# Every second feed-forward residue by ScalarE and an accumulating DMA

## The chip, the cores and the metric

The kernel runs on one core of a Trainium2 chip. A core has a matrix engine (TensorE, PE in the profile), a vector engine (VectorE, DVE), an engine for activation functions (ScalarE, ACT), a general engine (GpSimd, POOL), an engine that issues transfers (SyncE, SP) and sixteen DMA engines that carry them out. Each engine works through its own queue in order and waits for the others by semaphores. Operands lie in the on-chip memory SBUF, 128 partitions wide; TensorE sums into banks of the memory PSUM. The metric is the time of one execution on the device, in microseconds; less is better.

## The reference

One layer of a streaming encoder on 256 tokens of width 2048, in float32. Its first part (attention and a convolution, joined by an output projection w_out) is left out here; the change touches the last lines, the feed-forward part with a hidden width of 5632:

```python
h = h + jnp.einsum('bsm,md->bsd', mixed, w_out[l].astype(mixed.dtype))
hn = rms_norm(h, norm2_g[l])
a = jnp.einsum('bsd,df->bsf', hn, w_gate[l].astype(hn.dtype))
bu = jnp.einsum('bsd,df->bsf', hn, w_up[l].astype(hn.dtype))
h = h + jnp.einsum('bsf,fd->bsd', jax.nn.silu(a) * bu, w_down[l].astype(hn.dtype))
```

## The kernel before

All products run on TensorE in a type of reduced precision (float32r). To keep float32's precision, each operand is split into a rounded part and a residue, hi + lo, and each product is summed from three: hi·hi, lo·hi and hi·lo. For the weights this split is made on the chip, chunk by chunk.

A chunk is two k-tiles (128 rows each) of 512 columns of a weight matrix: 128 partitions of 1024 values, 512 KB. There are 377 chunks; 113 belong to the input and output projections and the last 264 to the feed-forward part (w_gate, w_up and w_down, 88 each). The function split_chunk does four things with a chunk: SyncE loads it from the chip's main memory into a tile raw (line 270; five buffers), ScalarE rounds it into whi (line 275), VectorE subtracts whi from raw into wlo (line 276), and the price of that subtraction is taken off a credit by which other VectorE work is spread over the stream. whi and wlo have four buffers each.

The function multiply issues a chunk's twelve products: for each k-tile and each half of the tokens, first the two with whi (lines 306 and 307, eight products, the first half), then the four with wlo (line 312, the second half). A block of chunks (eight for w_gate and w_up; twelve and ten for the two rounds of w_down) sums into the same two PSUM banks. After a block a generator takes the sums over: silu_done (ScalarE, line 713), up_done (VectorE line 721, transposes on TensorE line 729, split of the result by ScalarE line 732 and VectorE line 733), or down_done, which adds into h on VectorE (line 746) and, in the second round, stores the result by SyncE (line 748). The order on every queue is written out by hand; there is no scheduler.

The feed-forward part runs in two rounds: six column blocks of w_gate and w_up, then four passes over w_down (twelve chunks each); then five column blocks and four passes (ten chunks each). run_chunks keeps each engine's queue ahead of TensorE: before the products of chunk t are issued, the chunks up to t + lead(t) have been given to split_chunk. lead is 1 at the very start and AHEAD = 2 after it. A tile that comes round again makes its writer wait until the last reader of its old contents is done: the load of chunk i waits for the subtraction of chunk i − 5, the rounding of chunk i for the products of chunk i − 4.

Of the kernel before, what the change touches and what calls it, by code (L numbers as in the profile page):

```python
# [12 lines left out]
F32 = mybir.dt.float32  # L13
F32R = mybir.dt.float32r
AF = mybir.ActivationFunctionType
# [22 lines left out]

# where the rows of the gains and biases begin, 128 values to a row
ROWS = (("norm1_g", "g1", KD), ("norm2_g", "g2", KD), ("subln_g", "sg", 2),  # L40
# [4 lines left out]

# k-tiles of 512 columns in a chunk of weights
NK = 2
# transposes that warm the tensor engine up
WARM = (14, 5)
# how x comes in: the k-tiles of its parts  # L50
XPARTS = (range(0, 2), range(2, 4), range(4, 8), range(8, 12), range(12, 16))
# channel tiles of the convolution per block of products
CONV_BLOCKS = (1, 1, 2, 2, 2)
# chunks of weights that are split ahead of their products
AHEAD = 2
RAW_BUFS = 5
AUX = 4
# resumptions between the steps of the q and k rows
LAG = (3, 2, 6)
HL_BUFS = 4  # L60
# what the vector engine's filler may take per resumption, and the price of its work
KTILE_US = 1.30
TAP_US = 0.396
CHAIN_US = 0.127
LO_US = 0.568
# feed-forward column blocks between two passes of w_down
FGROUPS = (6, 5)


def rope_constants():  # L70
    """cos and signed sin of the rotary angles, [S, 2, DH]."""
    inv = np.float32(THETA) ** (-np.arange(0, DH, 2, dtype=np.float32) / np.float32(DH))
    ang = np.arange(S, dtype=np.float32)[:, None] * inv[None, :].astype(np.float32)
    c, s = np.cos(ang), np.sin(ang)
    return np.ascontiguousarray(
        np.stack([np.concatenate([c, c], -1), np.concatenate([-s, s], -1)], 1).astype(np.float32)
    )
# [3 lines left out]
def tile_block(  # L81
# [16 lines left out]

    # ---------------------------------------------------------------- inputs and constants
    h = [const.tile([P, D], F32, tag=f"h{m}", name=f"h{m}") for m in range(NM)]  # L100
# [5 lines left out]

    # the tensor engine's clock rises while the first loads are under way
    def warm_up(n):
# [7 lines left out]
    act.dma_start(out=rows, in_=gains)  # L116
    # a first use of the activation table before anything waits for it
    act.copy(small.tile([P, 8], F32, tag="rsq", name="first"), neghalf)
# [26 lines left out]
    def late_constants():  # L145
        late_loads()
        yield from lag(4)
        pw = aux_ps.tile([P, N], F32, tag="aux", name="ps_cw")
        for ct in range(NCT):
            pe.transpose(pw[:, ct * W : (ct + 1) * W], cw_rows[ct * P // N][:, ct * P % N : ct * P % N + P], ident[:W, :W])  # L150
        act.copy(cw.rearrange("p c w -> p (c w)"), pw[:, : NCT * W])
        while not normed:
            yield
        yield from lag(16)
        act.mul(cols[:, AT["sg"] : AT["sg"] + 2], cols[:, AT["sg"] : AT["sg"] + 2], 1.0 - LAMBDA_INIT)
        # q is scaled by 1/sqrt(d) through its gain
        act.mul(gb[:, 0, :], gb[:, 0, :], 1.0 / math.sqrt(DH))
        hd = DH // 2
        for i, key in enumerate("qk"):
            for m in range(NM):  # L160
                t = const.tile([P, 2, DH], F32, tag=f"gcs{key}{m}", name=f"gcs{key}{m}")
                pool.tensor_tensor(t[:, 0, :], rt[:, m, 0, :], gb[:, i, :], ALU.mult)
                pool.tensor_tensor(t[:, 1, :hd], rt[:, m, 1, :hd], gb[:, i, hd:], ALU.mult)
                pool.tensor_tensor(t[:, 1, hd:], rt[:, m, 1, hd:], gb[:, i, :hd], ALU.mult)
                gcs[key, m] = t
        lp = pre.tile([P, 2, DH], F32, tag="att", name="lp", bufs=4)
        for i in range(2):
            pool.tensor_tensor(lp[:, i, :], lamv[:, 2 * i, :], lamv[:, 2 * i + 1, :], ALU.mult)
        yield from lag(4)
        dve.tensor_reduce(ls, lp, AX.X, ALU.add)  # L170
# [3 lines left out]
    def negative_lambda():  # L174
        """-lambda = exp(l2) - exp(l1) - lambda_init"""
        le = const.tile([P, 2], F32, tag="le", name="le")
        act.activation(le, ls, AF.Exp)
        pool.tensor_tensor(neg_lam, le[:, 1:2], le[:, 0:1], ALU.subtract)
        pool.tensor_scalar(neg_lam, neg_lam, 1.0, -LAMBDA_INIT, ALU.mult, ALU.add)

    def rsqrt_mean(dst, ss, n, eps):
        """dst = (ss / n + eps) ** -0.5 on a few columns."""
        k = dst.shape[-1]
        t = small.tile([P, 8], F32, tag="rsq", name="rsq")
        pool.tensor_scalar(t[:, :k], ss, 1.0 / n, eps, ALU.mult, ALU.add)  # L185
        pool.tensor_tensor(dst, t[:, :k], neghalf[:, :k], ALU.pow)  # L186
# [6 lines left out]
    def split_scaled(pair, src, scale):  # L193
        """hi + lo = src * scale, src in PSUM."""
        hi, lo = pair
        act.activation(hi, src, AF.Copy, scale=scale)  # L196
        dve.scalar_tensor_tensor(lo, src, scale, hi.bitcast(F32), ALU.mult, ALU.subtract)  # L197

    # ---------------------------------------------------------------- the stream of products
    # Beside it run generators, resumed after each k-tile: what they emit between two yields  # L200
    # is ready when they are resumed, so that no engine waits in its queue.
    running = []
# [12 lines left out]

    # banks of the aux pool that are read in a later stage than they are written
    held = [0]
# [5 lines left out]

    # work of the vector engine that fills what the stream leaves free
    side = []
# [3 lines left out]
    def spend(us):  # L229
        credit[0] -= us  # L230
# [6 lines left out]
    def side_step():  # L237
        """One step of the two oldest chains by turns: a step waits for the one before it."""
        two = side[:2]
        turn[0] += 1  # L240
        q = two[turn[0] % len(two)]
        spend(TAP_US if len(two) > 1 else TAP_US + CHAIN_US)
        q.popleft()()
        if not q:
            side.remove(q)
# [4 lines left out]
    def block(w, cols, ks, xs, done=None, bkey=None, first=True, last=True, spare=False, cuts=()):  # L250
        """Products of the k-tiles ks with columns of w, summed in two banks."""
        ks = list(ks)
# [12 lines left out]
    def split_chunk(w, k0, nk, cols, width, **_):  # L265
# [9 lines left out]
        act.copy(hi, raw)  # L275
        dve.tensor_tensor(lo, raw, hi.bitcast(F32), ALU.subtract)  # L276
        spend(LO_US * nk * width / N)
        return hi, lo

    def operand(xs, k):  # L280
# [4 lines left out]
        return pair  # L285

    accs = {}

    def multiply(c, hi, lo):
# [24 lines left out]
        if c is chunks[-1]:  # L314
            # one half of the tokens after the other, which shortens the end
            for m in range(NM):
# [30 lines left out]

    # ---------------------------------------------------------------- x, its transpose
    xT = {}
# [38 lines left out]

    # ---------------------------------------------------------------- convolution channels
    NB = N // P  # L390
# [6 lines left out]
    def glu_done(c0, nct, ps):  # L397
        """ps holds the gates of nct channel tiles, then what they gate."""
        w = nct * P
# [38 lines left out]

    # layer norm with tokens on partitions, and back
    ytok = {}  # L440
# [4 lines left out]
    def conv_back(b):  # L445
# [20 lines left out]
        yield  # L466
        # the table of the silu below, ahead of need
        act.activation(small.tile([P, 8], F32, tag="rsq", name="first"), neghalf, AF.Silu)
# [32 lines left out]

    # ---------------------------------------------------------------- attention
    v_sb = [pre.tile([P, H * E], F32, tag=f"v{m}", name=f"v{m}", bufs=1) for m in range(NM)]
# [18 lines left out]
    def qk_rows(key, b, m, ps):  # L522
        """Norm and rotation of the heads of block b, and their transpose."""
        G = N // DH
# [31 lines left out]
    def attend_scores(hd):  # L556
# [62 lines left out]
        pe.transpose(pt[:, 2, :], wts[1][:, P:], ident)  # L619
        # in the place of the head's q, which is done with  # L620
        wT = qkT["q"][:, 2 * hd : 2 * hd + 2, :].rearrange("p g s -> p (g s)")[:, : 3 * P].rearrange("p (k s) -> p k s", k=3)
# [46 lines left out]

    # ---------------------------------------------------------------- output projection
    hT = {}  # L670
# [32 lines left out]

    # ---------------------------------------------------------------- feed-forward
    ffn = {}
# [44 lines left out]

    # ---------------------------------------------------------------- the order of it all
    QC, KC, VC, AC, GC = 0, 1024, 2048, 3072, 4096
# [25 lines left out]

    lead = lambda t: 1 if t < len(XPARTS) else AHEAD
    for c, part in enumerate(XPARTS):  # L780
# [29 lines left out]
```

## Time and profile before

| what | us |
|---|---|
| median of 2 runs (1091.94 to 1092.33) | 1092.13 |
| span of the profiled execution | 1089.8 |
| TensorE busy (PE) | 1079.0 |
| VectorE busy (DVE), of it line 276 | 647.1, 456.4 |
| ScalarE busy (ACT), of it line 275 | 509.6, 390.8 |
| GpSimd busy (POOL) | 49.1 |

The span runs from the first to the last instruction of the profiled execution. Its first 375 us hold the projections, the convolution and attention; from there on the feed-forward part runs. Busy times of different engines overlap, so they don't add up to the span. Lines of the profile name the line of the kernel, the engine, the operation, the tile written and the tiles read, the count, the time in all and the mean of one in ns, and then how long the engine stood idle before these instructions and what ended that. Idle time of an engine that isn't the bottleneck costs nothing by itself. In the table of windows the columns are the busy time of each engine with the number of instructions, TensorE's granted clock, the mean busy share of the sixteen DMA engines and the bytes that they moved.

### The profile page before, as it was taken

To read this page: it belongs to the slowest core of one execution; us is meant where nothing else is said; L and a number is where in the kernel's file an instruction comes from. 1 tells how busy PE (TensorE), PEld (TensorE's weight loads), DVE (VectorE), ACT (ScalarE), POOL (GpSimd) and SP (SyncE) were. 2 spreads that over 40 slices of the span, in tenths; PEclk is the share of its full clock that TensorE was granted. 3 is DMA by queue.
4 is the path that set the end of the run, shared out by engine and by line. 5 is a ranking of instruction groups with operands and counts; after the bars stand their busy time and mean duration, and the time that the engine had idled before them with its cause. 6 is when DMAs were issued, how large, how long until landed. Compare 5 with 4: busy or idle time off the path is not lost.

```text
span 1089.8 us, 13224 instructions
## 1 busy us (share of the span) xinstructions
PE 1079.0 (99%) x4952; PEld 894.0 (82%) x4952; DVE 647.1 (59%) x828; ACT 509.6 (47%) x719; POOL 49.1 (5%) x77
## 2 busy tenths in 40 slices
PE   8999999999999999999999999999999999999998
PEld 7988888877888888888888888888888888888886
DVE  4799989898766544544545454444454454544443
ACT  6644566755754544434444343333443444433332
POOL 0030112210100100000000000000000000000000
PEclk9999999999999999999999999999999999999999
DMA  8756665554456557666575555556666656653654
GB/s 241 233 177 198 190 189 161 154 169 155 155 181 206 174 172 220 187 192 189 168 214 184 192 192 193 192 187 190 194 186 192 189 169 211 186 192 108 219 204 146
DMA packets 118733, 203.02 MB, mean 186 GB/s; under 512 B 6932, under 2 KB 28878, under 8 KB 118668
## 3 DMA queue, kind: packets, MB, share of 16 engines
q1 hardware_dynamic: 118608, 202.14, 59.7%
q8 instruction: 39, 0.64, 0.2%
q14 instruction: 26, 0.21, 0.1%
q10 hardware_dynamic: 60, 0.03, 0.0%
HBM read 200.04 MB, written 2.10 MB: 185 GB/s over the span
## 4 chain that ended last, share of the span: by engine, by line
PE 92%; DVE 3%; ACT 2%; POOL 1%; issue 1%; DMA 1%; SPq 1%; DVEq 0%; ACTq 0%
PE acc L307 30%; PE acc L312 30%; PE acc L306 30%; DVE y L431 1%; DVE wlo L276 1%; PE ps_a L729 1%; ACT whi L275 1%; DMA h<-in_x_dram 1%; PE ps_o L643 1%; ACT junk L355 0%; POOL rsq L185 0%; PE ps_h L686 0%; SPq L360 0%; POOL fq L186 0%; SPq L270 0%
## 5 line engine op out<-in xcount | busy, mean ns | idle before, releaser
L276 DVE TENSOR_TENSOR wlo<-raw,whi 128x1024 fp32r<-128x1024 f32 (+1 forms) x377 | 456.4, 1221 | 337.3 <-ACT whi L275 304.5
L275 ACT CAST whi<-raw 128x1024 fp32r<-128x1024 f32 (+1 forms) x377 | 390.8, 1051 | 366.4 <-PE acc L307 326.6
L306 PE MATMUL acc<-whi,hhi 128*128 128x512 f32 x704 | 274.8, 390 | 0.0
L307 PE MATMUL acc<-whi,hlo 128*128 128x512 f32 x704 | 274.1, 389 | 0.0
L312 PE MATMUL acc<-wlo,hhi 128*128 128x512 f32 x704 | 189.2, 391 | 0.0
L307 PEld LDWEIGHTS acc<-whi,hlo 128*128 128x128 f32 x704 | 132.2, 188 | 27.3
L306 PEld LDWEIGHTS acc<-whi,hhi 128*128 128x128 f32 x704 | 132.2, 188 | 27.2
L312 PEld LDWEIGHTS acc<-wlo,hhi 128*128 128x128 f32 x704 | 131.4, 188 | 26.8
L306 PE MATMUL acc<-whi,ahi 128*128 128x512 f32 x384 | 150.7, 392 | 0.0
L307 PE MATMUL acc<-whi,alo 128*128 128x512 f32 x384 | 150.5, 392 | 0.0
L306 PE MATMUL acc<-whi,xhi 128*128 128x512 f32 (+1 forms) x352 | 130.0, 376 | 2.8 <-ACT xhi L196 2.8
L307 PE MATMUL acc<-whi,xlo 128*128 128x512 f32 (+1 forms) x352 | 128.6, 372 | 0.5 <-DVE xlo L197 0.4
L431 DVE SCALAR_TENSOR_TENSOR y<-upad,cw,y 128x256 f32<-128x256 f32 x240 | 103.6, 481 | 3.5 <-ACT y L424 3.0
L312 PE MATMUL acc<-wlo,ahi 128*128 128x512 f32 x384 | 103.6, 391 | 0.0
L312 PE MATMUL acc<-wlo,xhi 128*128 128x512 f32 (+1 forms) x352 | 88.7, 377 | 1.4 <-DVE wlo L276 1.2
L306 PEld LDWEIGHTS acc<-whi,ahi 128*128 128x128 f32 x384 | 72.1, 188 | 15.9
L307 PEld LDWEIGHTS acc<-whi,alo 128*128 128x128 f32 x384 | 72.1, 188 | 15.3
L312 PEld LDWEIGHTS acc<-wlo,ahi 128*128 128x128 f32 x384 | 71.9, 188 | 15.6
L306 PEld LDWEIGHTS acc<-whi,xhi 128*128 128x128 f32 x352 | 66.5, 189 | 14.7 <-ACT xhi L196 3.2
L307 PEld LDWEIGHTS acc<-whi,xlo 128*128 128x128 f32 x352 | 66.6, 189 | 11.9 <-DVE xlo L197 0.9
L312 PEld LDWEIGHTS acc<-wlo,xhi 128*128 128x128 f32 x352 | 62.3, 190 | 13.0 <-DVE wlo L276 2.2
L733 DVE TENSOR_TENSOR alo<-ps_a,ahi 128x512 fp32r<-128x512 f32 x22 | 15.2, 691 | 46.0 <-ACT ahi L732 46.0
(138 smaller groups left out, 544.2 us busy)
## 6 DMA issues: line engine op xcount, KB each, us to landing
raw<-in_w_gate_dram SPq DMA_DIRECT2D x88, 512.0 KB, 4.4
raw<-in_w_up_dram SPq DMA_DIRECT2D x88, 512.0 KB, 4.5
raw<-in_w_down_dram SPq DMA_DIRECT2D x88, 512.0 KB, 4.2
raw<-in_w_in_dram SPq DMA_DIRECT2D x48, 512.0 KB, 3.7
raw<-in_w_out_dram SPq DMA_DIRECT2D x32, 512.0 KB, 3.7
raw<-in_w_in_dram SPq DMA_DIRECT2D x62, 256.0 KB, 3.6
h<-in_x_dram SPq DMA_DIRECT2D x6, 256.0 KB, 6.1
out_dram<-h SPq DMA_DIRECT2D x6, 256.0 KB, 2.5
```

What stands on the lines that cost most here:

```text
L275: act.copy(hi, raw)
L276: dve.tensor_tensor(lo, raw, hi.bitcast(F32), ALU.subtract)
L306: pe.matmul(ps[m], xhi[:, ms], hi[:, j, :], start=c["first"] and j == 0, stop=False)
L307: pe.matmul(ps[m], xlo[:, ms], hi[:, j, :], start=False, stop=False)
L312: pe.matmul(ps[m], xhi[:, ms], lo[:, j, :], start=False, stop=c["last"] and j == nk - 1)
L431: dve.scalar_tensor_tensor(y[:, ct, :], src, wk, y[:, ct, :], ALU.mult, ALU.add)
L643: pe.matmul(o[:, m, :], wT[:, (0 if m == 0 else 1 + k), :], v_sb[k][:, hd * E : (hd + 1) * E], start=k == 0, stop=k == m)
L729: pe.transpose(pt[:, i, m * P : (m + 1) * P], aa[m][:, c : c + P], ident)
L733: dve.tensor_tensor(lo, pt, hi.bitcast(F32), ALU.subtract)
```

## The change

For the chunks of w_gate, w_up and w_down, every chunk with an odd number (132 of the 264) gets its residue in another way: ScalarE writes −raw, rounded as whi is, into wlo, and a transfer issued by GpSimd adds raw to it, in place, inside SBUF. The other chunks keep the subtraction. A list counts the chunks given to split_chunk, and the credit isn't charged where VectorE isn't used. The look-ahead of the feed-forward chunks goes from 2 to 3. The rest of the diff takes comments away and moves no line ahead of line 276.

```diff
@@ split_chunk
         act.copy(hi, raw)
-        dve.tensor_tensor(lo, raw, hi.bitcast(F32), ALU.subtract)
-        spend(LO_US * nk * width / N)
+        if len(ready_order) % 2 and any(w is t for t in (w_gate, w_up, w_down)):
+
+            act.activation(lo, raw, AF.Copy, scale=-1.0)
+            pool.dma_start(out=lo, in_=raw.bitcast(F32R), accum_op=ALU.add)
+        else:
+            dve.tensor_tensor(lo, raw, hi.bitcast(F32), ALU.subtract)
+            spend(LO_US * nk * width / N)
+        ready_order.append(k0)
         return hi, lo
...
+    ready_order = []
     accs = {}
...
-    lead = lambda t: 1 if t < len(XPARTS) else AHEAD
+    lead = lambda t: 1 if t < len(XPARTS) else AHEAD + any(chunks[t]['w'] is m for m in (w_gate, w_up, w_down))
```

## The prediction

> **What bounds the kernel now.** I read the page first, then the groups and waits of the feed-forward stretch, the timelines of ScalarE, SyncE and TensorE, and last the table of windows.
>
> ```profile
> span 1089.8 us, 13224 instructions
> ...
> PE 1079.0 (99%) x4952; PEld 894.0 (82%) x4952; DVE 647.1 (59%) x828; ACT 509.6 (47%) x719; POOL 49.1 (5%) x77
> ...
> PE   8999999999999999999999999999999999999998
> ...
> PEclk9999999999999999999999999999999999999999
> DMA  8756665554456557666575555556666656653654
> ```
>
> TensorE works in every slice, at full clock. The chain of waits says the same.
>
> ```profile
> PE 92%; DVE 3%; ACT 2%; POOL 1%; issue 1%; DMA 1%; SPq 1%; DVEq 0%; ACTq 0%
> PE acc L307 30%; PE acc L312 30%; PE acc L306 30%; DVE y L431 1%; DVE wlo L276 1%; PE ps_a L729 1%; ACT whi L275 1%; DMA h<-in_x_dram 1%; PE ps_o L643 1%; ACT junk L355 0%; POOL rsq L185 0%; PE ps_h L686 0%; SPq L360 0%; POOL fq L186 0%; SPq L270 0%
> ```
>
> The products hold 90% of the chain; the residue's subtraction (L276) holds 1%. The groups and the waits of 400 to 1080 us, all feed-forward, show what the two side engines do there.
>
> ```profile
> L276 DVE TENSOR_TENSOR wlo<-raw,whi 128x1024 fp32r<-128x1024 f32 x245 | 297.2, 1224 | 281.5 <-ACT whi L275 249.0 <-PE acc L307 30.9
> L275 ACT CAST whi<-raw 128x1024 fp32r<-128x1024 f32 x244 | 254.9, 1053 | 315.0 <-PE acc L307 284.2 <-DMA raw<-in_w_down_dram 30.2
> ...
> L713 ACT ACTIVATE sil<-acc,rstd 128x512 f32<-128x512 f32 x20 | 12.6, 684 | 21.2 <-PE acc L312 21.2
> ```
>
> ScalarE's rounding (1.05 us) waits for TensorE to give a buffer back, and VectorE's subtraction (1.22 us) waits for ScalarE: both idle because TensorE is slower. On ScalarE's timeline the period of one chunk can be read.
>
> ```profile
> 503.85 1.05 ACT L275 CAST whi<-raw 128x1024 fp32r<-128x1024 f32 x1 [1.67 <-PE acc L307]
> 506.57 1.05 ACT L275 CAST whi<-raw 128x1024 fp32r<-128x1024 f32 x1 [1.67 <-PE acc L307]
> ```
>
> One chunk takes 2.72 us (506.57 − 503.85), twelve products of 0.227 us. The feed-forward part has 264 chunks, 718 us.
>
> **Where the DMA engines stand.** The change moves data, so their room decides. The last passes over w_down show them at full pace: SyncE holds the next loads behind the stores of the output, then issues them at once.
>
> ```profile
> 1003.66 0.95 SPq L748 DMA_DIRECT2D out_dram<-h  x2
> 1004.71 13.30 SPq L270 DMA_DIRECT2D raw<-in_w_down_dram  x10
> ```
>
> ```profile
> 1009.89 1.05 ACT L275 CAST whi<-raw 128x1024 fp32r<-128x1024 f32 x1 [9.10 <-DMA raw<-in_w_down_dram]
> 1011.24 1.06 ACT L275 CAST whi<-raw 128x1024 fp32r<-128x1024 f32 x1 [0.29 <-DMA raw<-in_w_down_dram]
> ...
> 1015.30 1.05 ACT L275 CAST whi<-raw 128x1024 fp32r<-128x1024 f32 x1 [0.30 <-DMA raw<-in_w_down_dram]
> ```
>
> ```profile
> 375.00:1085.00 710.00, 710.00 (x3166) 586.19 (x3165) 346.38 (x314) 288.85 (x297) 0.00 (x0) 1.00 0.60 187
> ...
> 1010.00:1015.00 5.00, 5.00 (x23) 4.10 (x23) 3.68 (x3) 4.11 (x4) 0.00 (x0) 1.00 1.05 399
> ```
>
> Here ScalarE waits for the loads, which land every 1.35 us ((1015.30 − 1009.89) / 4); the windows' last two columns give 399 GB/s at a share of 1.05, against 187 GB/s and 0.60 over the whole part. So all sixteen engines together need 1.355 us for one 512 KB chunk at their best, and 0.60 × 2.72 = 1.63 us at their usual pace. Two chunks take TensorE 5.44 us and the loads 2.71 us: 2.73 us per pair are free.
>
> **The change, part by part.** *Removed:* one subtraction for every odd chunk of the feed-forward part: 132 × 1.224 = 162 us of VectorE. It held 1% of the chain, and VectorE idles 281 us in that part already. Gain: nothing, since TensorE is busy without a break.
>
> *Added on ScalarE:* 132 sign-reversed copies of 128x1024. Not in the trace; the nearest rows are the rounding, 1.05 us, and two silu rows, 2 × 0.684 = 1.37 us from PSUM. I take 1.05, as source and size are the rounding's. ScalarE then needs 3 × 1.05 = 3.2 us of each 5.44 and idled 315 us: hidden. The copy waits until the products of four chunks before have read the residue buffer. Behind it stands the next rounding, which waits for the following chunk's first half anyway, and at block ends the silu, about 1.05 us later, with a chunk or more before its reader.
>
> *Added on the DMA queues:* 132 transfers of 512 KB inside SBUF, issued by GpSimd, which has no work left there (0.00 in the window). No transfer of GpSimd is in the trace. Issue: SyncE's costs 0.37 us, and GpSimd's own small operations about 1.1 us; either is far under 5.44.
>
> ```profile
> L186 POOL TENSOR_TENSOR fq<-rsq,neghalf 128x4 f32<-128x4 f32 x8 | 9.0, 1131 | 0.7
> ```
>
> ```profile
> L270 SPq DMA_DIRECT2D raw<-in_w_gate_dram x7: 367/368/368, 513.2 to 528.0; - x7
> ```
>
> The engine time is the term that decides. An accumulation reads raw, reads the residue tile and writes it back. The lower end is one load's time, 1.355 us, if the second read costs nothing. For the upper end the stores from SBUF serve:
>
> ```profile
> out_dram<-h SPq DMA_DIRECT2D x6, 256.0 KB, 2.5
> ...
> out_dram<-h SPq DMA_DIRECT2D x4, 128.0 KB, 2.0
> ```
>
> 128 KB more take 0.5 us more, so 512 KB take 2.0 us, and three passes one after another 6.0 us. Between these: two passes at the load's best pace, 2.71 us, and three, 4.07 us. I take the middle of the last two, 3.39 us, because both reads must pass, and because the load's pace is this kernel's best and not its usual one. The pair then needs 2.71 + 3.39 = 6.10 us of DMA against 5.44 of TensorE: 0.66 us too much, × 132 = 87 us.
>
> The Trainium skill ("DMA: Bandwidth & Descriptors", Issuing engines are not separate DMA queues) says that DMAs of the scalar, sync and gpsimd engines run on the same 16 DMA engines and interleave. It speaks against the change; no run here yet shows a GpSimd transfer beside SyncE's.
>
> *Moved:* the look-ahead of the feed-forward chunks goes from 2 to 3, so loads, roundings and residues stand one chunk earlier in every queue; at the stores SyncE passes one load more before it waits. The hidden accumulation has this cover: the rounding starts once the first eight products of the fourth chunk before are done (8 × 0.227 = 1.81 us), rounding and copy end 2.1 us later, 1.2 us into the next chunk, and the residue is read 1.81 us into its own: 3 × 2.72 + 1.81 − 1.2 = 8.8 us are there. A load takes this long from issue to landing:
>
> ```profile
> DMA to landing us min/median/max: 3.4/4.4/8.6
> ```
>
> The raw buffer is held until the accumulation has landed, and SyncE's queue stands behind it: the load five chunks later, and all loads after it, wait.
>
> ```profile
> SPq L270 <- DVE wlo L276: 510.4, 225, 6.6
> ...
> SPq L748 <- DVE h L746: 42.3, 6, 14.9
> ```
>
> SyncE waited for the subtraction in 225 loads (up to 6.6 us) and nobody suffered; it will wait for the transfer in half of them.
>
> *At the last three stores* the cover is thin. TensorE starts the chunks after a pass at these times:
>
> ```profile
> 1003.20 0.39 PE L306 MATMUL acc<-whi,ahi 128*128 128x512 f32 x1
> ...
> 1011.44 0.39 PE L306 MATMUL acc<-whi,ahi 128*128 128x512 f32 x1
> ...
> 1014.18 0.39 PE L306 MATMUL acc<-whi,ahi 128*128 128x512 f32 x1
> ```
>
> The fourth chunk after the pass (1011.44) is the first held load now; its rounding ends at 1009.89 + 1.05 = 1010.94, 0.5 us early. After the change the fifth is the first held. Passes have ten chunks and end on even numbers, so the fifth is odd, an accumulated one. Its copy ends at 1009.89 + 2 × 1.05 = 1012.0, its residue is due at 1014.18 + 1.83 = 1016.0. Its transfer, 3.4 us plus the 2.0 us by which the shortest landing exceeds 1.355, plus 1.1 of issue, takes 6.5: 2.5 us late, three times, 8 us. That is the price wherever the cover above is gone.
>
> Sum against the profiled execution: 1089.8 + 87 + 8 = 1185 us of span; the median of the runs, 1092.1, is 2.3 above the span, so 1187 us.
>
> **The rivals.** *1, the engines have room (not slower).* If the accumulation costs two passes at the load's best pace, the pair needs 5.42 us, under 5.44, and nothing but the three store gaps shows: 1092 + 8 = 1100 us, or 1092 without them. It decides up to 2.9 us per accumulation (0.17 × 132 = 22 us, 2%). For it: 399 GB/s were reached, and SBUF rows need no HBM. Against it: it needs the sixteen engines at their best all the time. The Trainium skill ("Collectives: The Full Stack", The bandwidth ceiling) says that a reduce is slow only by its two source reads, not by the add; by that it is this case, two passes. Chance 0.35; 0.01 more that the new branch is never taken, 1092.
>
> *2, the accumulation is much dearer*, over 4.1 us, because passes do not overlap or the add is slow. At 6.0 us the pair needs 8.7 us: 3.27 × 132 = 432, 1532 us with the gaps and the launch. For it: nothing in the trace shows an add in a DMA. Chance 0.16.
>
> *3, a round trip that is too long though the engines have room.* A residue buffer comes back every fourth chunk, 10.88 us; less the copy 1.05 and its reading 0.91, 8.9 are left. With the longest landing, 8.6, and 1.1 of issue, 0.8 us are missing per four chunks: 66 × 0.8 = 53 us, 1145 us. Against it: the median landing is 4.4. Chance 0.03.
>
> *4, faster by over 2%* would need shorter products, and TensorE has no gap to give: 0.01.
>
> **How the numbers follow.** My forecast (the DMA engines become the bound, 2.9 to 4.1 us per accumulation) has 0.44 and its own range is 1114 (1092 + 22) to 1277 (4.07: 1.34 × 132 = 177, plus 8). 2% is about what a measurement of this kernel can tell from no change. Same: 0.36 (rival 1 and the untaken branch). Slower: 0.44 + 0.16 + 0.03 = 0.63. The range begins below rival 1 at 1088 and reaches to 5.4 us per accumulation, (2.71 + 5.4 − 5.44) × 132 = 352, to 1450; beyond it lies about half of rival 2.
>
> **What would show it.** Right: a DMA share near 1 from 375 us on, ScalarE's rounding waiting for raw loads in place of L307, the load's landing well above 4.4 us, L312 waiting for the accumulation, chunks of about 3.05 us, VectorE's L276 at 245 instead of 377 instructions. Wrong: a share of 0.8 to 0.95 with TensorE at 99%, which is rival 1; a share under 1 with L312 waiting is rival 3; TensorE below 80% is rival 2. If the copy takes well over 1.4 us or GpSimd's issue over 2 us, those terms were mis-sized.

## The result, and the profile after

| | before | after |
|---|---|---|
| median of the runs, us | 1092.13 | 1117.55 (1117.2 to 1117.9, 2 runs) |
| span of the profiled execution, us | 1089.8 | 1116.0 |
| ratio of the times, 95% interval | 1 | 1.0241 [1.0224, 1.0258] |

The change makes the kernel 2.4% slower. The direction was forecast, the size was not: 25 us were lost and 95 forecast. These are the lines of the page after that answer to those shown of before. Line 276 is now 281, the copy is 278, the transfer 279, and the products' lines 306, 307 and 312 are 313, 314 and 319.

```profile
span 1116.0 us, 13501 instructions
...
PE 1089.1 (98%) x4952; PEld 895.4 (80%) x4952; DVE 488.4 (44%) x696; ACT 636.1 (57%) x851; POOL 159.0 (14%) x209
...
PE   8999999999999999999999999999999999998987
...
DMA  8756655544557999999999999999999999999995
...
q1 hardware_dynamic: 118608, 202.14, 52.9%
q0 software_dynamic: 19008, 69.21, 33.1%
...
PE 67%; DMA 20%; ACT 4%; DVE 4%; issue 3%; POOL 1%; SPq 1%; ACTq 0%; DVEq 0%
...
L279 POOL DMA_DIRECT2D wlo<-raw x132 | 114.1, 864 | 693.6 <-ACT wlo L278 678.7
...
L278 ACT ACTIVATE wlo<-raw 128x1024 fp32r<-128x1024 f32 x132 | 139.0, 1053 | 11.5 <-PE acc L319 11.5
...
wlo<-raw POOLq DMA_DIRECT2D x132, 512.0 KB, 7.1
raw<-in_w_gate_dram SPq DMA_DIRECT2D x88, 512.0 KB, 7.1
```

VectorE lost 159 us of work (647.1 − 488.4) and nobody gained by it. The DMA engines, 0.6 busy before, are busy for nine tenths or more in all but the first and the last slice of the feed-forward part, and a gate load lands 7.1 us after its issue in place of 4.4 (medians). Still TensorE is almost as busy as before until the 37th slice, which begins at 1004 us. The two rows of the wait table for its weight loads, asked for 375 to 985 us and for 985 us to the end, say what it waits for; the columns are the sum, the number and the longest.

```profile
PEld acc L319 <- DMA wlo<-raw: 13.6, 19, 1.5
```

```profile
PEld acc L319 <- DMA wlo<-raw: 11.6, 4, 4.2
```

It waits for the accumulated residue alone: nineteen short waits in 610 us, then four with the longest at 4.2 us. To see what each part cost, I read from the trace when TensorE begins the first feed-forward chunk (its first weight load, at 353.7 us before and 353.4 after), the 130th chunk (after one gate and one up block of the feed-forward part) and the 338th (the last forty, whose passes end in stores). From the first feed-forward chunk to the 130th is "entry", from there to the 338th "steady", then to the last product "last passes".

| kernel (profiled execution) | entry | steady | last passes | more than before |
|---|---|---|---|---|
| before | 44.5 | 576.5 | 111.2 | |
| after | 45.9 | 586.4 | 126.4 | 1.4 + 9.9 + 15.2 |

So two separate losses have to be explained: about 11 us spread over entry and steady part, and 15 us in the last 126.

**A late landing in the steady part.** In the groups of GpSimd, in the windows and on the timeline of TensorE's weight loads, one of the nineteen waits looks like this (the accumulated chunk that TensorE begins at 556.67):

```profile
550.37 0.86 POOL L279 DMA_DIRECT2D wlo<-raw  x1 [4.51 <-ACT wlo L278]
```

```profile
551.00:553.00 2.00, 2.00 (x10) 1.69 (x9) 0.00 (x0) 0.78 (x1) 0.23 (x1) 1.00 1.03 372
553.00:555.00 2.00, 2.00 (x10) 1.65 (x10) 1.23 (x1) 1.75 (x3) 0.00 (x0) 1.00 0.91 205
```

```profile
559.78 0.77 PEld L319 LDWEIGHTS acc<-wlo,hhi 128*128 128x128 f32 x4 [1.33 <-DMA wlo<-raw]
```

GpSimd is done with the issue at 551.23. The DMA engines are full (1.03, 0.91), but with something else: by the packet records of the two queues, from 551.23 to 555.1 they begin 526 packets of loads, two loads' worth, and none of the accumulation. Its last packet ends at 559.3, and it counts as landed 9.4 us after the issue began. TensorE could have used it from 558.45 on, 8.1 us after the issue began, and waits 1.33 us. These 8.1 us are also the median of what the order of work leaves an accumulation in the steady part, from the start of its issue until it is due.

**A stall at a store.** The chain of waits, in order of time (start, duration, what), around the first stall of the last passes:

```profile
1021.74 0.93 PE acc L319 x4
...
1023.71 1.06 ACT wlo L278
1024.77 0.28 issue
1025.06 5.84 DMA wlo<-raw
1030.89 0.04 issue
1030.94 2.07 PE acc L319 x4
```

The accumulation (5.84 us) ends the wait. Then the same four products take 2.07 us that took 0.93 before the wait: the granted clock is half of full for 3.41 us from 1030.5 on. It drops so three times, at 1030.5, 1064.6 and 1095.3. From the first weight load after each of the three long waits to the same one of the next chunk it takes 3.97, 4.22 and 4.01 us in place of 2.75: some 4.0 us for the clock. The waits of the weight loads are 11.6 us in this part (4.1, 4.2, 2.8 and 0.4), so together they make up the 15.2, 0.4 us over, since every wait holds a little of the usual gap.

### The profile page after: what moved, and what is told of

Its sections match the earlier page's. It is cut to its first block, busy times and chain, and to the rows that moved or that the text cites. A ratio compares the mean times of both kernels' runs of the same rounds, so it can differ in the third digit from the quotient of the medians.

```text
span 1116.0 us, 13501 instructions
## 1 busy us (share of the span) xinstructions
PE 1089.1 (98%) x4952; PEld 895.4 (80%) x4952; DVE 488.4 (44%) x696; ACT 636.1 (57%) x851; POOL 159.0 (14%) x209
## 4 chain that ended last, share of the span: by engine, by line
PE 67%; DMA 20%; ACT 4%; DVE 4%; issue 3%; POOL 1%; SPq 1%; ACTq 0%; DVEq 0%
PE acc L319 22%; PE acc L314 21%; PE acc L313 21%; DMA wlo<-raw 13%; DMA raw<-in_w_down_dram 4%; ACT wlo L278 2%; DMA raw<-in_w_gate_dram 1%; DVE wlo L281 1%; DVE y L438 1%; ACT whi L275 1%; PE ps_a L736 1%; DMA raw<-in_w_up_dram 1%; DMA h<-in_x_dram 1%; PE ps_o L650 1%; ACT junk L362 0%
## 5 line engine op out<-in xcount | busy, mean ns | idle before, releaser
L281 DVE TENSOR_TENSOR wlo<-raw,whi 128x1024 fp32r<-128x1024 f32 (+1 forms) x245 | 298.0, 1221 | 546.3 <-ACT whi L275 546.0
L279 POOL DMA_DIRECT2D wlo<-raw x132 | 114.1, 864 | 693.6 <-ACT wlo L278 678.7
L319 PEld LDWEIGHTS acc<-wlo,hhi 128*128 128x128 f32 x704 | 130.2, 188 | 37.1 <-DMA wlo<-raw 11.3
L278 ACT ACTIVATE wlo<-raw 128x1024 fp32r<-128x1024 f32 x132 | 139.0, 1053 | 11.5 <-PE acc L319 11.5
L319 PE MATMUL acc<-wlo,ahi 128*128 128x512 f32 x384 | 106.9, 401 | 10.7 <-DMA wlo<-raw 10.7
```

The lines of the kernel that those rows point to most:

```text
L278: act.activation(lo, raw, AF.Copy, scale=-1.0)
L279: pool.dma_start(out=lo, in_=raw.bitcast(F32R), accum_op=ALU.add)
L319: pe.matmul(ps[m], xhi[:, ms], lo[:, j, :], start=False, stop=c["last"] and j == nk - 1)
```

## The experiments

Two theories stood against the prediction's bandwidth theory once its size had failed. **Round trip:** the engines have room, but single accumulations land later than four buffers allow. **Held loads:** in the last passes the loads stand behind the stores, and the first of them is an accumulated chunk's. All kernels below start from the changed one unless said otherwise; each was timed against the kernel before, which took 1091.1 to 1091.4 us on these chips.

**What one accumulation costs the engines.** All residues accumulated, and a plain copy in the accumulation's place:

```diff
-        if len(ready_order) % 2 and any(w is t for t in (w_gate, w_up, w_down)):
+        if any(w is t for t in (w_gate, w_up, w_down)):
```

> All 264 feed-forward residues go through the accumulating transfer, so the DMA engines must become the bound and the time gives the engine time of one accumulation. Two passes at the load's best pace (2.7 us): chunks of 1.355 + 2.7 = 4.05 us, 264 x (4.05 - 2.72) = 351 us more than before, about 1443 us. The prediction's 3.39 us: chunks of 4.74 us, 534 us more, about 1626 us. Three passes (4.07 us): about 1806 us.

```diff
-            pool.dma_start(out=lo, in_=raw.bitcast(F32R), accum_op=ALU.add)
+            pool.dma_start(out=lo, in_=raw.bitcast(F32R))
```

> The odd chunks' transfer copies raw over the residue instead of adding it, so it reads one operand and not two; the residue is not computed. If the second read is what an accumulation costs beside a copy, a 4 KB packet takes about 164 ns in place of the 328 ns seen in the changed kernel, the pair of chunks needs 2.7 + 1.3 = 4.0 us of 5.44, the DMA share falls to about 0.8, the small waits of the steady part go (11 us) and the gaps at the three stores shrink by about 1.3 us each: 1097 to 1104 us. If the add or the path inside SBUF is the dear part and not the second read, packets stay well above 200 ns and the time stays above 1110.

Measured: 1395.3 us with all accumulated (ratio 1.2789 [1.2748, 1.2831]), under all three expected times, and 1099.5 us with the copy (1.0074 [1.0059, 1.0089]), as expected. The pages' rows of GpSimd's queue (packets, MB, share of 16 engines), of the former and the latter:

```profile
q0 software_dynamic: 38016, 138.43, 51.3%
```

```profile
q0 software_dynamic: 19008, 69.21, 18.2%
```

Before, a feed-forward chunk takes 2.77 us in the mean, transposes and w_down included ((44.5 + 576.5 + 111.2) / 264). With all accumulated it takes 2.77 + (1395.32 − 1091.16) / 264 = 3.92 us, of which one accumulation can hold no more than 3.92 − 1.355 = 2.6 us. By the packets' time it is 0.513 × 1392.6 / 264 = 2.71 us, and 0.331 × 1116.0 / 132 = 2.80 in the changed kernel; a copy takes 0.182 × 1098.3 / 132 = 1.51. An accumulation costs a little under two copies; whether the second read or the add is the dear part, these two runs don't separate. That is the first rival's price, not the 3.39 us of the forecast: a load pair and an accumulation need at most 2.71 + 2.6 = 5.3 us of TensorE's 5.44. With the copy, steady part and entry lose nothing (44.5 and 576.4) and the last passes still 9.0 us.

**Room to land.** Three ways to give more buffers:

> Seven raw buffers in place of five, seven pairs of whi and wlo in place of four (from the memory that is free in the feed-forward part) and a look-ahead of five chunks in place of three; the same transfers. Round trip theory: the engines have room (two passes, 5.4 of 5.44 us), and the loss comes from single accumulations that land 8 to 9 us after their issue, where four buffers leave about 8.1; with two more chunks of cover the stalls go, in the steady part and at the stores: 1092 to 1095 us. Bandwidth theory: the pair really needs over 5.44 us; deeper buffers only delay the first stall, the steady part still loses about 11 us: 1102 us or more.

The edit of the second way, five pairs, in parts:

```diff
-RAW_BUFS = 5
+RAW_BUFS = 3
...
-HL_BUFS = 4
+HL_BUFS = 5
...
+        own = "pool" in ffn and len(ready_order) % 9 in (0, 1, 3, 4, 6, 7)
+        raw = view(ffn["pool"].tile([P, NK * N], F32, tag="fraw", name="raw", bufs=6) if own
+                   else wp.tile([P, NK * N], F32, tag="raw", name="raw", bufs=RAW_BUFS))
...
-... AHEAD + any(chunks[t]['w'] is m for m in (w_gate, w_up, w_down))
+... AHEAD + (1 + ('pool' in ffn)) * any(chunks[t]['w'] is m for m in (w_gate, w_up, w_down))
```

> Five pairs of whi and wlo in place of four, at the same place in memory (three raw buffers there and six from free memory in the feed-forward part), and a look-ahead of four chunks: an accumulation has 2.7 us more to land, at the same transfers and the same pace of the products (2.72 us a chunk). Round trip theory: the steady stalls (11 us) and the three at the stores (15 us with the clock) go, 1092 to 1096 us. Bandwidth theory: the steady part still loses about 11 us, 1102 us or more.

> Nine raw buffers in place of five, all else as in the changed kernel. If accumulations are late because SyncE is held by the raw buffer that an accumulation still reads and then issues two or three loads in a burst, ahead of the next accumulation, the bursts go and most of the 11 us of the steady part: 1105 to 1110 us, with the store gaps unchanged. If the DMA engines simply serve what was issued first, more loads stand ahead of each accumulation and it gets no better: 1115 us or more.

| run | time, us | ratio, interval | entry, steady, last passes: more than before |
|---|---|---|---|
| seven pairs, elsewhere in memory | 1109.2 | 1.0167 [1.0152, 1.0183] | 2.8 + 8.6 + 6.7 |
| five pairs, same place | 1106.2 (1101.8 to 1107.4) | 1.0128 [1.0106, 1.0150] | 3.8 + 0.0 + 6.1 |
| nine raw buffers alone | 1131.4 | 1.0354 [1.0317, 1.0391] | 4.3 + 11.5 + 27.1 |

The times of the runs with seven and with five pairs both lie where the bandwidth theory had them, and for other reasons. With seven pairs, from 400 to 985 us the weight loads never wait for a residue; but the chunks of w_gate and w_up themselves take longer: 2.79 us for the odd ones, whose whi and wlo lie in the other place, and 2.75 for the even, against 2.72. A slower TensorE also leaves the DMA engines more time, so that run decides nothing. The run with five pairs keeps the operands where they were and the pace at 2.72. Windows of 400 to 980 us, first the changed kernel, then this one (the last columns are clock, DMA share and GB/s):

```profile
400.00:980.00 580.00, 574.71 (x2550) 469.75 (x2549) 157.88 (x151) 336.03 (x349) 88.58 (x103) 1.00 1.01 279
```

```profile
400.00:980.00 580.00, 580.00 (x2593) 479.45 (x2592) 162.80 (x155) 341.08 (x356) 90.37 (x105) 1.00 1.03 288
```

The same transfers at a DMA share of 1.03, and TensorE is busy for all 580 us: the steady loss is gone to the tenth. The landings of the accumulations in these windows, in the same order:

```profile
DMA to landing us min/median/max: 5.2/7.2/9.4
```

```profile
DMA to landing us min/median/max: 4.9/7.9/10.5
```

They come no earlier with five pairs, but they now have 10.9 us in the median and not 8.1. It was the round trip and not the bandwidth. (The profiled execution was the shortest of four, so the other runs may wait somewhere else too. The fifth pair and the fourth chunk of look-ahead were not tried apart.) What is left of the loss lies in the entry and the last passes.

The other raw buffers are not what helped: nine of them with four pairs made it worse, by little in the steady part (11.5 us against 9.9) and by much at the stores (27.1 against 15.2). After a store SyncE now issues nine loads one right after another, where the changed kernel issues five and then waits for a buffer, and the longest wait for a residue grows to 7.4 us. That fits "served in the order of issue". The bursts of held loads in the steady part this run did not take away: SyncE still waits for an accumulation at 108 loads there, 466.5 us in all (changed kernel: 108, 403.9), so it doesn't tell what they cost.

**The stores.** ScalarE issues them (sp.dma_start becomes act.dma_start for out):

> The stores of the output are issued by ScalarE, so SyncE's loads do not stand behind them. If the last passes lose their 15 us because the loads are held behind the stores (three stalls of 2.4 to 3.8 us on the accumulated residue and three drops of the granted clock after them), these go and the clock stays at 0.998: about 1102 us. If the last passes lose time because the DMA engines cannot keep up there, it stays at 1115 to 1118.

1107.0 us, 1.0147 [1.0132, 1.0163], 5 us more than expected. Entry and steady part stay as they were (1.8 + 9.5), the last passes lose 4.1 us in place of 15.2, and the clock doesn't drop. So the loads held behind the stores are the second loss; some 4 us are left because the waits for late residues go on there:

```profile
PEld acc L319 <- DMA wlo<-raw: 4.7, 4, 1.7
```

The even chunks in place of the odd ones:

> The even chunks are accumulated in place of the odd ones. The first load held behind a store then belongs to a subtracted chunk, and the accumulated one after it has 2.7 us more for 1.4 us more of loading. If the store gaps come from the accumulation's time on the first held chunk, they shrink by at least 1.3 us each and the clock drops go with most of them: 1105 to 1112 us. If not, 1115 to 1119.

1112.5 us, 1.0194 [1.0177, 1.0211]. Just outside the expectation, and not by the way expected: the last passes still lose 13.6 us with two clock drops. The accumulated chunk is now the second held one, and its stall after the first two of these stores shrinks as forecast, to 2.6 and 2.9 us from 4.1 and 4.2; but other waits come in, and the sum of the waits stays (11.3 us against 11.6). What improved is the steady part, 3.8 us in place of 9.9, for which I have no explanation.

**The look-ahead.** Left at 2 with the rest of the change, and at 3 in the kernel before, without accumulation:

> The look-ahead stays at 2 as before, the rest of the change stands. SyncE passes one load fewer before each store, and the silu of a block stands ahead of the next rounding. The accumulated chunk after a store gets its load 1.4 us later in the row of held loads: stalls of about 5 us in place of 3.3, 1121 to 1127 us in all. If the third chunk of look-ahead has no part in it, 1116 to 1119.

> The kernel before with the look-ahead of 3 in the feed-forward part and no accumulation. No theory gives it a cost or a gain: TensorE has no gap there to fill, 1090 to 1093 us. Over 1095 would mean that a part of the loss is the look-ahead's.

1150.6 us (1.0547 [1.0531, 1.0563]) and 1091.1 us (1.0001 [0.9992, 1.0010]). The look-ahead costs nothing by itself, and the change needs it: without it the steady part loses 32 us and the last passes 26. The expectation (1121 to 1127) looked at the stores alone and missed the steady part, where an accumulation one chunk later in every queue is late again and again: 31 waits of up to 2.5 us from 400 to 985 us, some for accumulations that are issued only 4.1 us before they are due.

**Everything at once, and half of it.** Five pairs, stores by ScalarE, and the longer look-ahead and the first accumulation only once the new buffers exist (three accumulations fewer); and, by itself, every fourth residue in place of every second:

> As the run with five pairs of whi and wlo, but with the stores issued by ScalarE, and with the longer look-ahead and the first accumulation only once the feed-forward buffers exist (two or three accumulations fewer). If the loss of the changed kernel is the sum of late landings in the steady part and of the loads held behind the three stores, nothing is left: 1092 to 1095 us. If the engines lack bandwidth anywhere, or accumulations slow the products, some of it stays: 1098 us or more.

> Every fourth residue is accumulated (66 in place of 132). Four chunks then need 4 x 1.355 + 2.7 = 8.1 us of the DMA engines against 10.9. Waiting behind loads shrinks with the load on the engines, so the steady part loses 0 to 3 us; of the three stores only the second has an accumulated chunk as the first held one (3.5 us and 1.7 us for the clock): 1093 to 1100 us. If each accumulation had a cost of its own, half of the loss stays: 1104 us.

1098.1 us (1.0064 [1.0047, 1.0081]), 3 us over what the sum of the two losses gave: the steady part loses nothing and the last passes 0.7 us, but the entry 5.0. The timelines of GpSimd and of the weight loads show where:

```profile
366.68 1.08 POOL L281 DMA_DIRECT2D wlo<-raw  x1
```

```profile
376.61 1.35 PEld L321 LDWEIGHTS acc<-wlo,hhi 128*128 128x128 f32 x4 [3.80 <-DMA wlo<-raw]
```

The first accumulation of all is issued at 366.7 and landed only before 376.6; SyncE issues eight loads from 362.1 on, now that the six new buffers exist. By the packet records they stand ahead of it: between the end of its issue (367.76) and its first packet (371.64) 567 packets of loads begin. The wait of 3.8 us is followed by another drop of the clock, at 376.0; the two make the 5.0. With every fourth residue accumulated, 1099.3 us (1.0075 [1.0057, 1.0092]): nothing lost at entry and in the steady part, 8.0 at the stores, with stalls at two of them where I expected one.

**The changed kernel again:**

> The changed kernel again, beside the runs of this group on one chip: 1115 to 1120 us, with the same two parts in the trace, about 11 us in the steady part and 15 us from the first store on.

1120.8 us (1116.3 to 1123.9), 1.0266 [1.0237, 1.0295], with 1.3 + 8.6 + 15.4 us: both losses come back at the same places. No version here beats the kernel before; TensorE's own pace leaves them nothing to win.

## Why the prediction was right and wrong

**Right.** TensorE is the bound, and 159 us less of VectorE's work are worth nothing. The copy takes 1.053 us (1.05 taken) and is hidden. GpSimd's issue takes 0.86 us, between the two bounds given. The loads held behind the last three stores stall TensorE on the fifth chunk, an accumulated one, each time.

**The step that failed: the engine time of an accumulation.** "I take the middle of the last two, 3.39 us", and from it 87 us. It measured at most 2.6 us by the pace of the run with all residues accumulated, 2.7 to 2.8 by the packets' time. The lower of the two values between which I chose, two passes at the load's best pace (2.71 us), was close, and with it the first rival's sum, 5.42 of 5.44 us. The other side of the comparison was a little off too: 5.44 us is a pair of gate chunks without the transposes between blocks, and in the steady part a pair takes 5.54 us (576.5 / 104), so even 3.39 us would have given 74 us and not 87. With the right price the sum would have been the first rival's 1100 us; the other 17 or so are the next two paragraphs. The Trainium skill ("Collectives: The Full Stack", The bandwidth ceiling), which puts a reduce's price in its two source reads, agrees with 2.80 us against 1.51 for a copy, though the runs don't show the add apart from the read.

**What took its place: the third rival's mechanism**, to which I gave 0.03. I put the cover at 8.8 us from the end of the copy, where the changed kernel leaves 8.1 from the start of the issue in the median, and argued with the median landing of a load before, 4.4 us. That median belonged to a queue 0.6 full. With the accumulations in it, it became about 7 us, for loads and accumulations alike, up to 9.4 us for an accumulation, and some came too late: 11 us, where that rival's price was 53. It had 0.8 us missing in every four chunks; here nineteen accumulations were late, by at most 1.5. What I told as two cases, room or no room, is one: engines that are nearly full serve everybody, but late.

**The stores' term was mis-sized: 8 us, measured 15.** The stall was to be 2.5 us and was 4.1, 4.2 and 2.8. The first transfer took 5.8 us from its issue where 6.5 was reckoned, but its copy ended only 2.0 us ahead of the due time (1024.77 against 1026.81, when the weight loads of the first half are done) and not 4.0. The timelines of VectorE and SyncE at that pass show why:

```profile
1014.62 1.23 DVE L281 TENSOR_TENSOR wlo<-raw,whi 128x1024 fp32r<-128x1024 f32 x1 [4.28 <-ACT whi L275]
1015.76 1.28 DVE L753 TENSOR_TENSOR h<-h,acc 128x512 f32<-128x512 f32 x2
```

```profile
1016.47 0.96 SPq L755 DMA_DIRECT2D out_dram<-h  x2
1017.52 17.48 SPq L270 DMA_DIRECT2D raw<-in_w_down_dram  x9
```

With the look-ahead of 3 one more subtraction stands ahead of the addition whose result is stored. So the store starts 2.45 us after the first weight load of the next pass (1016.47 − 1014.02) where it was 0.68 (1003.66 − 1002.98), and the held loads with it. It is the look-ahead: the store starts 2.45 us into the pass with the look-ahead of 3 alone too, and 0.68 with accumulations and the look-ahead of 2. I had named that everything stands one chunk earlier in every queue, and not followed it to VectorE's addition. And the clock, which drops after each of these stalls, was in no term: some 4.0 us.

**The signs I named.** A DMA share near 1 came, and I had tied it to my forecast; it came with at most 5.3 of 5.44 us of need. The later landings and the waits for the accumulation came too; chunks of 3.05 us did not, and the raw loads took the place of TensorE only in part in what the rounding waits for (123 us, against 139 for the first halves of chunks, from 375 us on). The share counts the time that packets are under way and passes 1 without any loss (1.03 in the run with five pairs). The sign that would have told was who waits, and for how long: nineteen waits of at most 1.5 us are a queue's lateness, and not a missing bandwidth, which would be paid in every pair.

## What to carry to other kernels

Work taken off an engine that isn't the bound is worth nothing, and a transfer put in its place is paid by everyone who shares the DMA engines: near full, each transfer lands later, so ask first how many buffers cover the landing time under the new load, not the old. Price an accumulating transfer at two copies, and look for the place where loads are held up and then catch up at full pace; there the shared engines have no room at all. Where an order is written out by hand, a longer look-ahead moves work ahead of everything else in a queue, so follow each queue to what now stands behind it.

## What the runs showed of the hardware

- **A transfer starts behind what the other queue was given before it.** In the case above 526 packets of loads began, and none of an accumulation whose issue was over, in 3.9 us; once it had begun, its 128 packets went out among 245 of loads. Over all 132 accumulations of the changed kernel the first packet began 0.56 us after the end of the issue at the earliest, 1.18 us in the median and 4.46 at the latest; with every fourth residue accumulated, and few loads in the way, the median was 0.57. The Trainium skill ("DMA: Bandwidth & Descriptors", Queues, rings and completion order) says that each engine goes round its queues packet by packet, where a packet is typically 9 to 17 descriptors. If a packet record of the profile is one descriptor, the 526 are 33 for each engine, so more than one such turn passed; the trace doesn't show which engine took which.
- **The clock drops on a fixed grid, after a stretch in which TensorE was busy for less than some 0.45.** In each of the fourteen profiles, from 30 us on, all drops begin whole multiples of 3.413 us apart and last one or more such stretches at half of full. Divided by that grid, the stretches at full clock that a drop followed (51) had TensorE busy for 0.45 or less, by the profile's records; of the other 4357 none was under 0.44. So a wait counts by how it lies: in the changed kernel one of 2.8 us lay mostly in one stretch, which left it 0.43 busy, and the clock dropped; one of 3.1 us in the run with five pairs was spread over two, 0.72 and 0.49, and it did not. The Trainium skill ("TensorE: Matmul & The Clock Gate", Part 1: The HAM clock gate) has windows of about 3.4 us; the length agrees.
- **A product's time seems to depend on where its operands lie.** Chunks took 2.75 and 2.79 us in the run with seven pairs, against 2.72 in the changed kernel's gate and up blocks. In the kernel before, the chunks of w_down, whose other operand lies elsewhere, took 2.747. No run moves an operand and nothing else, so the cause is not shown.
